# Low halves of the second feed-forward weights from an accumulating transfer instead of a VectorE subtraction

## The chip, the cores and the metric

The kernel runs on one core of a Trainium2 chip. The core has five engines that each follow their own instruction queue: TensorE (PE, matrix products), VectorE (DVE), ScalarE (ACT), GpSimd (POOL) and SyncE (SP, which here only issues transfers). Transfers run on 16 DMA engines. The metric is the device time of one execution in microseconds (us). Before the change it is 1752.12 us, the median of three runs (1749.69 to 1752.14).

## The reference

The program is a two-layer diffusion backbone in 32-bit floats: 256 latent tokens and 256 context tokens of width 1024. Each layer is a feed-forward sub-layer, an attention sub-layer (latent attention in layer 0, windowed attention in layer 1) and a second feed-forward sub-layer. Cut to what matters here:

```python
def swiglu(h, w_in, w_out):                    # w_in: 1024 x 5632, w_out: 2816 x 1024
    g, u = jnp.split(h @ w_in, 2, axis=-1)
    return (jax.nn.silu(g) * u) @ w_out
...
x  = x  + 0.5 * gate_x * swiglu(modulate(rms_norm(x),  shift_x, scale_x), w_in, w_out)
xc = xc + 0.5 * gate_c * swiglu(modulate(rms_norm(xc), shift_c, scale_c), w_in, w_out)
```

Shift, scale and gate come from two conditioning vectors by a product with large modulation weights. The context stream (xc) is not needed after the attention of layer 1, so the last of the four feed-forward sub-layers works on 256 columns (one stream) instead of 512 (two).

## The kernel before

**Three products for one.** A 32-bit operand is held as two tiles, hi (the operand rounded to a shorter float that PE reads at full rate) and lo (operand minus hi). A product is hi·hi + hi·lo + lo·hi, three matmuls per term (`mm3`, lines 205 to 214; the matmuls are L210, L211 and L212, and only L212 reads the weight's lo half).

**A weight tile's way.** SP loads 128 rows of 1024 or 896 floats (512 or 448 KB) into a raw tile (`weight_raw`, L191, name wraw, 3 buffers in a ring). ACT rounds it into whi (L182, a cast, 4 buffers). DVE subtracts, wlo = wraw - whi (L183, 4 buffers); in some attention places POOL does that instead. PE then reads whi and wlo. A buffer of wraw is free for the next load once the subtraction has read it; a buffer of whi or wlo once PE has used it. `weight` and `weight_split` do this for every weight of the program.

**A feed-forward sub-layer** (`ffn`) goes through three groups of 8, 7 and 7 blocks of the 2816 inner columns. For each block, two weight tiles of 1024 columns (in_win) give the gate and the up half; ACT computes the silu (L416), DVE the product (L418), and ACT and DVE split it into hi and lo (the tiles called r2k in the profile). Then comes the group's `closing`: eight tiles of the second weight (in_wout), one per 128 output rows, each 1024 columns wide in the first group and 896 in the others, so 24 or 21 matmuls per tile. DVE adds each result to the residual (L357). In the last group of a two-stream sub-layer the last two tiles are held and computed one stream after the other; the squares for the next norm are taken by ACT (L236) and added up on POOL (L242).

**Background work.** Beside the first three feed-forward sub-layers, modulation vectors are computed in small steps (`pump`): SP loads 512 KB tiles (modraw, L146, 2 buffers), DVE multiplies and adds them into accumulators (L149, L151, 1024 columns each), and PE sums over partitions (L157). There are none beside the last feed-forward sub-layer.

**What sets the order.** A scheduler puts each engine's instructions into one fixed order when the program is built, and inserts the waits; on the chip each engine follows its order, and a waiting instruction holds up those behind it. Tiles of one name share a ring of buffers, and an instruction that writes to a buffer waits until its former contents have been used.

Of the kernel before, what the change touches and what calls it, by code (L numbers as in the profile page):

```python
# [10 lines left out]
F32 = mybir.dt.float32  # L11
F32R = mybir.dt.float32r
# [5 lines left out]
P = 128  # L18
# [19 lines left out]
def hybrid_backbone_kernel(ctx, tc, t, out):  # L38
# [23 lines left out]

# [1 line left out]
    def load_const(name, shape, dtype=F32):  # L64
# [26 lines left out]

# [1 line left out]
    def mod_columns(l, psA, rows, blocks, dests):  # L93
        """psA [rows, 128 * blocks] has values in row off, for each (off, stream, first column) of dests,
        that belong to the d-tiles from that column on."""
        sA = tmp()
        nc.scalar.copy(sA[:rows, :blocks * P], psA[:rows, :blocks * P])
        yield
        psB = bank()
        vB = psB.rearrange("p (b r) -> p b r", r=P)  # L100
        for b in range(blocks):
            nc.tensor.transpose(vB[:, b, :rows], sA[:rows, b * P:(b + 1) * P], ident[:rows, :rows])  # L102
        for off, s, col in dests:
            nc.vector.tensor_tensor(mod[l][:, s, col:col + blocks], vB[:, :blocks, off], modb[:, l, col:col + blocks], ALU.add)
# [9 lines left out]
    def load_column(k):  # L114
        """Both of layer 0's first chunks for d-tile k, as halves of the rows."""
        raws = [[], []]
        for i in range(2):
            for c in range(2):
                raw = r2k().bitcast(F32)
                nc.sync.dma_start(raw, t["modo"][k, c, i])  # L120
                raws[c].append(raw.rearrange("p (k n) -> p k n", k=4))
        return raws
# [40 lines left out]
    def behind(ins):  # L163
        """Queues a block's instructions of ins's engine behind ins."""
        return tc.issue_after(ins.ins) if ins else nullcontext()
# [11 lines left out]

# [1 line left out]
    def split(hi, lo, src, bias=None, engine=nc.vector):  # L179
        """hi + lo = src (+ bias), each with 12 significant bits."""  # L180
        if bias is None:
            nc.scalar.copy(hi, src)  # L182
            return engine.tensor_tensor(lo, src, hi.bitcast(F32), ALU.subtract)  # L183
        else:
            nc.scalar.activation(hi, src, AF.Identity, bias=bias)  # L185
            return nc.vector.scalar_tensor_tensor(lo, src, bias, hi.bitcast(F32), ALU.add, ALU.subtract)  # L186
# [10 lines left out]
    def weight_split(raw, engine=nc.vector, after=None):  # L197
# [5 lines left out]
        return hi[:, :n], lo[:, :n]  # L203

    def mm3(o, terms, which=None, n=None):
        """o = sum over the n terms of lhsT.T @ rhs, operands given as (hi, lo) pairs; or which terms of it."""
        n = n or len(terms)
        for i in range(n) if which is None else which:
            (ah, al), (bh, bl) = terms[i]
            nc.tensor.matmul(o, lhsT=ah, rhs=bh, start=(i == 0), stop=False)  # L210
            nc.tensor.matmul(o, lhsT=ah, rhs=bl, start=False, stop=False)  # L211
            nc.tensor.matmul(o, lhsT=al, rhs=bh, start=False, stop=(i == n - 1))  # L212
# [4 lines left out]
    def rstd_of(parts, dim, after=None):  # L217
        """1 / sqrt(sum over parts / dim + eps) on every partition; parts are tiles of squares."""
        b = bank()[:, :T]
        for i, p in enumerate(parts):  # L220
            nc.tensor.matmul(b, lhsT=ones, rhs=p, start=(i == 0), stop=(i == len(parts) - 1))
        r = strip()
        nc.scalar.activation(r, b, AF.Sqrt, scale=1.0 / dim, bias=eps)  # L223
        with behind(after):
            nc.vector.reciprocal(r, r)  # L225
        return r

    class Squares:
        """The sum of the squares of all tiles but the last, and the last one's."""

# [13 lines left out]
    def load_table(func, q):  # L244
        """Has ScalarE load func's table as soon as q, a tile of squares, is there."""
        d = small(1)
        nc.scalar.activation(d, q[:, 0:1], func, scale=1.0 if func == AF.Sqrt else -1.0)

    class Sublayer:
        """The modulated input of a sub-layer, one stream after the other, and its first weights."""  # L250

# [58 lines left out]
        def leading(self, s):  # L310
            """The products of the prefetched tiles with one stream, in the order in which its input gets ready,
            and those of the other first tiles."""
            self.product(self.lead[:self.both], s)
            if len(self.streams) > 1 and s == 0:
                self.r[1] = self.rstd(1)
            for i in range(self.both, len(self.first)):
                if i == len(self.lead):
                    ap, size = self.first[i]
                    self.lead.append((weight(ap, size, after=self.end), bank(), size // KT))
                self.product(self.lead[i:i + 1], s)  # L320
# [6 lines left out]
        def products(self, specs):  # L327
            """One bank per weight tile: first the prefetched ones, then the others."""
            for i, (ap, size) in enumerate(specs):
# [10 lines left out]
    class Final(Sublayer):  # L340
        """The final norm of the latent stream."""

# [16 lines left out]

    def closing(tiles, chunk, l, streams, nxt, tail, per_tile=0):  # L360
        """x += gate * product, for each (weight, size, inputs); the last tiles one stream after the other,
        so that the next sub-layer's norm of the first stream runs beside the second's products."""
        w = T * len(streams)
# [5 lines left out]
        for d in range(KT - tail):  # L369
            pump(per_tile)  # L370
            ap, inputs = tiles[d]
            wt = weight(ap, len(inputs) * P)
            o = bank()
            mm3(o[:, :w], terms(wt, inputs, slice(0, w)))
            residual(l, chunk, d, o, streams)
            for s in streams:
                if nxt:
                    nxt.grown(s, d)
# [19 lines left out]

# [1 line left out]
    def ffn_specs(l, which):  # L400
        return [(t["win"][l, which, f, u], 1024) for f in range(NF) for u in range(2)]

    def ffn(sl, nxt, per_tile=0):
# [4 lines left out]
        for g, (f0, f1) in enumerate(GROUPS):  # L408
            gu = []
            for f in range(f0, f1):  # L410
# [12 lines left out]
            closing([(t[f"wout{g}"][l, which, d], gu) for d in range(KT)], 2 + 6 * which, l, streams,  # L423
                    nxt if last else None, 2 if last else 0, per_tile // 2)

# [1 line left out]
    def spread(like, x):  # L427
        return x.rearrange("p (i c) -> p i c", i=2) if len(like.shape) == 3 else x

    def block(e, b):  # L430
        """The b-th block of 128 keys."""
        return e[:, b // 2, b % 2 * P:(b % 2 + 1) * P] if len(e.shape) == 3 else e[:, b * P:(b + 1) * P]
# [5 lines left out]
    def softmax(os, scale, place, sink=None, minus_sink=None):  # L438
        """For each (o, w): exp(scale * o) / (sum of that over a row, and of exp(sink))."""
        n = len(os)  # L440
# [23 lines left out]
    def transposed(es, k0):  # L464
        """Blocks k0 and k0 + 1 of the keys of two query tiles -> (hi, lo) [keys, (block, query)]."""
        b = bank()
# [7 lines left out]
    class Rope:  # L474
        """R[:, :T] = rope of q[:, :T]: the split first, so that its product can come later."""

# [17 lines left out]
    class StackedRope(Rope):  # L494
        """The same of two heads' q, each head's split stacked already."""

# [4 lines left out]
    def stack(dst, R, half, engine=nc.vector):  # L501
        """dst [128, n]: rows of R's half as (hi; lo) for half 0, (lo; hi) for half 1."""
        a = slice(64 * half, 64 * half + 64)
# [12 lines left out]
    def pipeline(n, project, rope, scores, turn, apply, q, e, at={}):  # L516
        """Head h's softmax and splits run beside the products of the heads next to it."""
        for h in range(n):
# [10 lines left out]

# [1 line left out]
    def mla_specs():  # L531
        return [(t["wdown"][m], 1024) for m in (4, 5, 0)] + [(t["wkr"], 512)] + [(t["wdown"][m], 1024) for m in range(1, 4)]

    def mla(sl, nxt):
# [3 lines left out]
        class Normed:  # L538
            """RMS norm of the tiles, as pairs."""

# [153 lines left out]

# [1 line left out]
    def swa(sl, nxt):  # L696
# [47 lines left out]
        def scores(m, *qs):  # L744
# [13 lines left out]
            heads = slice(2 * m, 2 * m + 2)  # L758
            # The context's residual is not needed any more.
            place = (lambda j: tmp()) if m % 2 else (lambda j: x_all[:, 2 * j:2 * j + 2, C])  # L760
# [39 lines left out]

# [1 line left out]
    def load_tmp(name, n):  # L802
# [39 lines left out]
    def lead_products(n, k1):  # L842
        """Those of the first n leading weight tiles with the d-tiles before k1."""
        for k in range(k1):
# [57 lines left out]
def _layout(x, c, ctx, c_ctx, mod_w, mod_b, norm_g, final_norm_g, ffn_w_in, ffn_w_out, mla_w_down, mla_q_norm,  # L902
# [9 lines left out]
    def tiles(w, m):  # L912
        """(K, M * m) -> [M, 128, K / 128, m]: each column tile with its K on partitions."""
        k, n = w.shape
# [63 lines left out]
```

## Time and profile before

| | |
|---|---|
| runs, median (lowest to highest) | 1752.12 us (1749.69 to 1752.14) |
| profiled execution, span from first to last instruction | 1747.8 us |
| median of the runs above that span | 4.3 us |
| PE busy | 1686.9 us, 97% |
| DVE busy | 1093.9 us, 63% |
| ACT busy | 659.6 us, 38% |
| POOL busy | 188.1 us, 11% |
| subtractions for wlo on DVE | 302, 361.6 us |
| mean granted TensorE clock | 0.989 |

The profile is of one execution. "Busy" counts an engine's instructions; a matmul's record overlaps with the next one's, so that PE's pace is better read from the distance between tiles than from the length of one record. A group of the profile stands for all instructions of one line with the same operands: its name gives line, engine, operation, output<-input and shape, then the count, busy time and mean in ns, and after the second bar the idle time of the engine just before them and what ended it. A window's row gives the busy time and the count for each engine in a stretch of time, then the granted clock, the busy share of the DMA engines and what they moved.

### The profile page before, as it was taken

The page shows a single profiled execution, that of the slowest core. Times are in us where ns is not written, and L with a number is a line of the kernel's source. Part 1 is how long each engine was busy: PE and PEld are TensorE (multiplying, and loading weights), DVE is VectorE, ACT ScalarE, POOL GpSimd, SP SyncE. Part 2 cuts the span into 40 slices and gives each one's busy share as a digit, 9 for nine tenths or more (in the row PEclk, how much of TensorE's full clock was granted, in tenths as well). Part 3 has the DMA queues.
Part 4 walks back from the last instruction along what each step waited for, and adds up shares of the span by engine and source line. Part 5 has one row for each costly group of instructions (what it writes and reads, how often), then busy time and mean ns, then how long its engine had stood idle before and what let it go on. Part 6 is the DMA issues. An engine that isn't in the chain of part 4 may idle for free.

```text
span 1747.8 us, 23827 instructions
## 1 busy us (share of the span) xinstructions
PE 1686.9 (97%) x9428; PEld 1438.3 (82%) x9428; DVE 1093.9 (63%) x1608; ACT 659.6 (38%) x1105; POOL 188.1 (11%) x183
## 2 busy tenths in 40 slices
PE   7999999999999999999999999999999989889997
PEld 4688888888788898888888888888888878889997
DVE  4877576646767467856946474635433689755554
ACT  4422222234556353222222342222222566554443
POOL 1000000004132130000000220000000452110001
PEclk9999999999999999999999999999999999999998
DMA  9566455431212126644645245635323221145552
GB/s 340 172 199 192 129 192 179 158 120 55 85 49 73 51 84 201 209 143 155 219 128 166 92 158 168 217 119 159 96 97 94 88 85 37 62 145 181 173 191 95
DMA packets 72831, 242.71 MB, mean 139 GB/s; under 512 B 8848, under 2 KB 10640, under 8 KB 72720
## 3 DMA queue, kind: packets, MB, share of 16 engines
q1 hardware_dynamic: 72720, 241.20, 42.6%
q8 instruction: 74, 1.21, 0.3%
q14 instruction: 37, 0.30, 0.1%
HBM read 240.11 MB, written 1.05 MB: 138 GB/s over the span
## 4 chain that ended last, share of the span: by engine, by line
PE 54%; DVE 5%; issue 1%; ACT 1%; POOL 1%; DMA 0%; POOLq 0%; ACTq 0%; DVEq 0%
PE bank L210 18%; PE bank L211 18%; PE bank L212 18%; DVE small L444 1%; DVE r2k L183 1%; DVE x L461 1%; PE bank L157 1%; DVE tmp L461 0%; DVE wlo L183 0%; DVE strip L225 0%; DVE r2k L506 0%; DVE r2k L512 0%; PE bank L102 0%; POOL r2k L183 0%; DVE small L448 0%
## 5 line engine op out<-in xcount | busy, mean ns | idle before, releaser
L210 PE MATMUL bank<-r2k,whi 128*128 128x512 f32 (+1 forms) x2610 | 918.4, 353 | 9.2 <-ACT r2k L185 4.6
L211 PE MATMUL bank<-r2k,whi 128*128 128x512 f32 (+1 forms) x2610 | 915.5, 351 | 8.1 <-POOL r2k L183 5.7
L212 PE MATMUL bank<-r2k,wlo 128*128 128x512 f32 (+1 forms) x2610 | 912.8, 350 | 4.2 <-POOL wlo L183 2.2
L182 ACT CAST whi<-wraw 128x1024 fp32r<-128x1024 f32 (+1 forms) x313 | 321.6, 1028 | 887.6 <-PE bank L211 527.5
L210 PEld LDWEIGHTS bank<-r2k,whi 128*128 128x128 f32 x2610 | 495.2, 190 | 89.6 <-ACT whi L182 9.2
L211 PEld LDWEIGHTS bank<-r2k,whi 128*128 128x128 f32 x2610 | 496.7, 190 | 76.8 <-POOL r2k L183 8.0
L212 PEld LDWEIGHTS bank<-r2k,wlo 128*128 128x128 f32 x2610 | 496.2, 190 | 69.3 <-POOL wlo L183 3.1
L183 DVE TENSOR_TENSOR wlo<-wraw,whi 128x1024 fp32r<-128x1024 f32 (+1 forms) x302 | 361.6, 1199 | 135.1 <-ACT whi L182 124.9
L151 DVE SCALAR_TENSOR_TENSOR big<-modraw,conds,big 128x1024 f32<-128x1024 f32 x196 | 242.4, 1279 | 11.3 <-DMA modraw<-in_modw 10.7
L357 DVE SCALAR_TENSOR_TENSOR x<-bank,mod,x 128x256 f32<-128x256 f32 x192 | 85.7, 478 | 181.7 <-PE bank L212 181.6
L242 POOL TENSOR_TENSOR strip<-strip 128x256 f32<-128x256 f32 x64 | 66.3, 1049 | 1137.0 <-ACT strip L236 1110.3
L418 DVE TENSOR_TENSOR tmp<-bank,tmp 128x512 f32<-128x512 f32 (+1 forms) x88 | 54.9, 623 | 180.3 <-PE bank L212 178.5
L183 DVE TENSOR_TENSOR r2k<-bank,r2k 128x512 fp32r<-128x512 f32 (+2 forms) x107 | 61.1, 615 | 15.6 <-ACT r2k L182 15.3
L182 ACT CAST r2k<-bank 128x512 fp32r<-128x512 f32 (+2 forms) x107 | 51.5, 545 | 15.2 <-PE bank L212 14.8
L183 DVE TENSOR_TENSOR r2k<-tmp,r2k 128x512 fp32r<-128x512 f32 (+1 forms) x88 | 54.3, 618 | 1.5 <-ACT r2k L182 1.4
L182 ACT CAST r2k<-tmp 128x512 fp32r<-128x512 f32 (+1 forms) x88 | 49.7, 566 | 9.7 <-DVE tmp L418 9.2
L416 ACT ACTIVATE tmp<-bank 128x512 f32<-128x512 f32 (+1 forms) x88 | 47.3, 537 | 6.5 <-PE bank L212 6.5
L444 DVE TENSOR_REDUCE small<-bank 128x1 f32<-128x512 f32 (+1 forms) x64 | 37.2, 612 | 0.2 <-PE bank L640 0.2
L236 ACT ACTIVATE strip<-x 128x256 f32<-128x256 f32 x80 | 30.5, 410 | 17.9 <-DVE x L357 17.0
L225 DVE RECIPROCAL strip<-strip 128x256 f32<-128x256 f32 x14 | 24.5, 1750 | 19.9 <-ACT strip L223 19.9
L186 DVE SCALAR_TENSOR_TENSOR r2k<-r2k,mod 128x256 fp32r<-128x256 f32 x45 | 29.9, 688 | 8.8 <-ACT r2k L185 8.6
L450 ACT ACTIVATE tmp<-bank,small 128x512 f32<-128x512 f32 x32 | 21.8, 687 | 30.1 <-DVE small L448 13.0
(150 smaller groups left out, 1057.2 us busy)
## 6 DMA issues: line engine op xcount, KB each, us to landing
wraw<-in_win SPq DMA_DIRECT2D x172, 512.0 KB, 3.5
modraw<-in_modw SPq DMA_DIRECT2D x128, 512.0 KB, 4.2
wraw<-in_wout SPq DMA_DIRECT2D x64, 448.0 KB, 3.3
wraw<-in_wout SPq DMA_DIRECT2D x32, 512.0 KB, 3.5
r2k<-in_modo SPq DMA_DIRECT2D x32, 256.0 KB, 5.8
wraw<-in_mwo SPq DMA_DIRECT2D x8, 512.0 KB, 3.5
wraw<-in_swq SPq DMA_DIRECT2D x8, 512.0 KB, 3.4
wraw<-in_swo SPq DMA_DIRECT2D x8, 512.0 KB, 3.4
```

The costliest lines, as they stand in the source:

```text
L151: nc.vector.scalar_tensor_tensor(acc[s], raw, conds[:, kt, s:s + 1], acc[s], ALU.mult, ALU.add)
L182: nc.scalar.copy(hi, src)
L183: return engine.tensor_tensor(lo, src, hi.bitcast(F32), ALU.subtract)
L210: nc.tensor.matmul(o, lhsT=ah, rhs=bh, start=(i == 0), stop=False)
L211: nc.tensor.matmul(o, lhsT=ah, rhs=bl, start=False, stop=False)
L212: nc.tensor.matmul(o, lhsT=al, rhs=bh, start=False, stop=(i == n - 1))
L236: nc.scalar.activation(q, x, AF.Square)
L242: nc.gpsimd.tensor_tensor(self.parts[0], self.parts[0], q, ALU.add)
L357: nc.vector.scalar_tensor_tensor(xs[d][:, SL[s]], o[:, SL[s]], mod[l][:, s, c:c + 1], xs[d][:, SL[s]], ALU.mult, ALU.add)
L416: nc.scalar.activation(sg[:, :w], og[:, :w], AF.Silu)
L418: nc.vector.tensor_tensor(pr[:, :w], ou[:, :w], sg[:, :w], ALU.mult)
L444: nc.vector.tensor_reduce(top[:, j:j + 1], o[:, :w], axis=AX.X, op=ALU.max)
```

## The change

A second way of making a weight's pair is added, `weight_added`, and the closings of the feed-forward sub-layers use it for all tiles that are not held: 4 x 3 x 8 less 3 x 2, which is 90 tiles (32 of 1024 columns, 58 of 896). ACT casts raw into whi as before; ACT then writes -whi into wlo; then POOL issues a transfer that adds the raw tile onto wlo. The result is again raw - whi. All other weights keep the subtraction. Comments and docstrings are dropped, and what stands below line 204 moves down by 10 lines: the matmuls are L220, L221 and L222 afterwards, the residual L367, the silu L426, the square L246, the adds of squares L252.

```diff
+    def weight_added(ap, n=1024):
+
+        raw = weight_raw(ap, n)
+        hi = ring.tile([P, 1024], F32R, tag="whi", name="whi", bufs=4)
+        lo = ring.tile([P, 1024], F32R, tag="wlo", name="wlo", bufs=4)
+        nc.scalar.copy(hi[:, :n], raw)
+        nc.scalar.mul(lo[:, :n], hi[:, :n].bitcast(F32), -1.0)
+        nc.gpsimd.dma_start(lo[:, :n].bitcast(F32), raw, accum_op=ALU.add)
+        return hi[:, :n], lo[:, :n]
...
-    def closing(tiles, chunk, l, streams, nxt, tail, per_tile=0):
+    def closing(tiles, chunk, l, streams, nxt, tail, per_tile=0, added=False):
...
-            wt = weight(ap, len(inputs) * P)
+            wt = (weight_added if added else weight)(ap, len(inputs) * P)
...
             closing([(t[f"wout{g}"][l, which, d], gu) for d in range(KT)], 2 + 6 * which, l, streams,
-                    nxt if last else None, 2 if last else 0, per_tile // 2)
+                    nxt if last else None, 2 if last else 0, per_tile // 2, added=True)
```

The scheduler's order of the loads on SP, in the second group of the last feed-forward sub-layer. What an instruction waits for stands in brackets: DMAHW is an earlier load, DMASW an earlier accumulating transfer, the other names are engines (the number behind belongs to the semaphore's name). Before:

```order
L191 DMA wraw<-in_wout 128x896 [waits DMAHW0_49,DVE_49]
L191 DMA wraw<-in_wout 128x896 [waits DMAHW1_49,DVE_49]
L191 DMA wraw<-in_wout 128x896 [waits DMAHW2_49,DVE_49]
L191 DMA wraw<-in_wout 128x896 [waits DMAHW3_49,DVE_49]
L191 DMA wraw<-in_wout 128x896 [waits DMAHW4_49,DVE_49]
```

And with the change:

```order
L191 DMA wraw<-in_wout 128x896 [waits DMAHW0_49,DVE_49]
L191 DMA wraw<-in_wout 128x896 [waits DMAHW1_49,DVE_49]
L191 DMA wraw<-in_wout 128x896 [waits DMAHW2_49,DVE_49]
L191 DMA wraw<-in_wout 128x896 [waits DMAHW3_49,DMASW2_49,Activation_49]
L191 DMA wraw<-in_wout 128x896 [waits DMAHW4_49,DMASW3_49,Activation_49]
```

The order of the loads is the same; from the fourth tile on, a load into a raw buffer waits for an accumulating transfer (DMASW) where it waited for DVE.

ACT's order at the same place, where the last two blocks' silu and split run beside the closing's first weights. Before:

```order
L182 CAST whi<-wraw 128x896
L416 ACTIVATE tmp<-bank 128x256
L182 CAST whi<-wraw 128x896
L182 CAST r2k<-tmp 128x256
L182 CAST whi<-wraw 128x896
L416 ACTIVATE tmp<-bank 128x256
L182 CAST whi<-wraw 128x896
L182 CAST r2k<-tmp 128x256
```

And with the change:

```order
L210 CAST whi<-wraw 128x896
L426 ACTIVATE tmp<-bank 128x256
L211 ACTIVATE wlo<-whi 128x896
L210 CAST whi<-wraw 128x896
L182 CAST r2k<-tmp 128x256
L211 ACTIVATE wlo<-whi 128x896
L210 CAST whi<-wraw 128x896
L426 ACTIVATE tmp<-bank 128x256
L211 ACTIVATE wlo<-whi 128x896
L210 CAST whi<-wraw 128x896
L182 CAST r2k<-tmp 128x256
```

A negation (L211) stands behind every cast of a second weight (now L210), and the silu (L426) and the split of the last blocks (the casts into r2k) stand between them as before.

## The prediction

> **What bounds the kernel now.** I read the busy times first, then the groups of instructions by shape, then the table of windows, then single stretches of the timeline.
>
> ```profile
> span 1747.8 us, 23827 instructions
> PE 1686.9 (97%) x9428; PEld 1438.3 (82%) x9428; DVE 1093.9 (63%) x1608; ACT 659.6 (38%) x1105; POOL 188.1 (11%) x183
> ...
> q1 hardware_dynamic: 72720, 241.20, 42.6%
> ...
> L183 DVE TENSOR_TENSOR wlo<-wraw,whi 128x1024 fp32r<-128x1024 f32 (+1 forms) x302 | 361.6, 1199 | 135.1 <-ACT whi L182 124.9
> ...
> wraw<-in_wout SPq DMA_DIRECT2D x64, 448.0 KB, 3.3
> wraw<-in_wout SPq DMA_DIRECT2D x32, 512.0 KB, 3.5
> ```
>
> PE is busy for 97% of the span; all its idle time is 1747.8 - 1686.9 = 60.9 us. The 302 subtractions on DVE look like a large target, but what counts is whether PE waits for them:
>
> ```profile
> L212 PE MATMUL bank<-r2k,wlo 128*128 128x512 f32 x1606 | 626.8, 390 | 4.2 <-POOL wlo L183 2.2 <-DVE wlo L183 2.0
> L211 PE MATMUL bank<-r2k,whi 128*128 128x256 f32 x996 | 286.1, 288 | 7.2 <-POOL r2k L183 5.7 <-DVE r2k L186 1.4
> L212 PE MATMUL bank<-r2k,wlo 128*128 128x256 f32 x996 | 282.9, 285 | 0.0
> ```
>
> In the whole program PE waits 2.0 us for a low half from DVE. The second feed-forward weights (tensors in_wout) are used in twelve closings; the windows show nine of them. Columns: busy time (and count) of PE, weight load, DVE, ACT, POOL, then clock, DMA share, GB/s.
>
> ```profile
> 131.00:176.00 45.00, 45.00 (x205) 36.30 (x204) 32.48 (x43) 9.45 (x11) 0.00 (x0) 1.00 0.61 193
> 256.00:294.00 38.00, 38.00 (x171) 31.46 (x170) 30.89 (x42) 7.88 (x9) 0.00 (x0) 1.00 0.67 206
> 722.00:767.00 45.00, 45.00 (x205) 36.30 (x204) 32.97 (x43) 9.64 (x10) 0.00 (x0) 1.00 0.61 197
> 847.00:885.00 38.00, 38.00 (x171) 31.41 (x170) 31.29 (x43) 7.62 (x10) 0.00 (x0) 1.00 0.64 204
> 1103.00:1147.00 44.00, 44.00 (x196) 35.23 (x195) 22.78 (x33) 8.60 (x9) 1.06 (x1) 1.00 0.56 181
> 1226.00:1264.00 38.00, 38.00 (x170) 31.19 (x169) 15.13 (x26) 7.41 (x8) 0.65 (x1) 1.00 0.33 101
> 1592.00:1614.00 22.00, 21.98 (x184) 21.77 (x183) 13.15 (x17) 7.87 (x8) 0.00 (x0) 1.00 0.55 178
> 1655.00:1675.00 20.00, 19.98 (x167) 19.77 (x166) 13.15 (x17) 7.75 (x9) 0.00 (x0) 1.00 0.60 191
> 1715.50:1735.50 20.00, 19.97 (x163) 19.36 (x161) 9.59 (x14) 6.62 (x13) 6.05 (x6) 1.00 0.20 65
> ```
>
> PE is full in every one of them, so a lighter DVE has nothing to give there. The question is only whether the new path is fast enough. The pace it must hold is read from the residuals, one per tile; the first rows are from a two-stream closing, the others from the last, one-stream, feed-forward:
>
> ```profile
> 756.65 0.88 DVE L357 SCALAR_TENSOR_TENSOR x<-bank,mod,x 128x256 f32<-128x256 f32 x2 [3.35 <-PE bank L212]
> 762.09 0.88 DVE L357 SCALAR_TENSOR_TENSOR x<-bank,mod,x 128x256 f32<-128x256 f32 x2 [3.36 <-PE bank L212]
> ...
> 1593.43 0.48 DVE L357 SCALAR_TENSOR_TENSOR x<-bank,mod,x 128x256 f32<-128x256 f32 x1 [0.60 <-PE bank L212]
> 1596.31 0.48 DVE L357 SCALAR_TENSOR_TENSOR x<-bank,mod,x 128x256 f32<-128x256 f32 x1 [0.64 <-PE bank L212]
> ...
> 1659.15 0.94 ACT L182 CAST whi<-wraw 128x896 fp32r<-128x896 f32 x1 [1.45 <-PE bank L211]
> 1659.23 0.48 DVE L357 SCALAR_TENSOR_TENSOR x<-bank,mod,x 128x256 f32<-128x256 f32 x1 [0.41 <-PE bank L212]
> 1660.12 1.09 DVE L183 TENSOR_TENSOR wlo<-wraw,whi 128x896 fp32r<-128x896 f32 x1 [0.41 <-ACT whi L182]
> 1661.75 0.48 DVE L357 SCALAR_TENSOR_TENSOR x<-bank,mod,x 128x256 f32<-128x256 f32 x1 [0.53 <-PE bank L212]
> ```
>
> A tile takes PE 5.44 us with two streams (7/8 of it, 4.76, where the tile has 896 columns), but with one stream 2.88 us (1024 columns) or 2.52 us (896). ACT casts a tile when PE frees its slot of whi: with 4 slots, three tiles ahead of PE.
>
> **The change part by part.** *Removed:* 90 of the 302 subtractions on DVE, about 90 x 1.2 = 107 us of DVE. Worth 0: PE waits 2.0 us for all 302 together, and not in these windows. *Added on ACT:* 90 negations as wide as the cast. The trace has none; its nearest rows are the cast itself and an activation and a cast of equal width:
>
> ```profile
> L182 ACT CAST whi<-wraw 128x1024 fp32r<-128x1024 f32 x248 | 260.6, 1051 | 682.0 <-PE bank L211 431.3 <-issue 221.0 <-DMA wraw<-in_win 22.1
> L182 ACT CAST whi<-wraw 128x896 fp32r<-128x896 f32 x64 | 60.4, 944 | 205.6 <-issue 109.5 <-PE bank L211 96.1
> L182 ACT CAST r2k<-tmp 128x512 fp32r<-128x512 f32 x66 | 41.0, 622 | 9.7 <-DVE tmp L418 9.2
> L416 ACT ACTIVATE tmp<-bank 128x512 f32<-128x512 f32 x66 | 38.9, 589 | 6.5 <-PE bank L212 6.5
> ```
>
> So between 0.95 and 1.0 of the cast; I take the cast's 1.05 and 0.94 us. ACT goes from 7.75 to about 15.3 of 20 us in the window at 1655: not full. *Added on POOL and the DMA engines:* 90 accumulating transfers of 448 or 512 KB, from the raw tile into the negated one, issued by POOL. POOL is 11% busy, and its adds of squares, which now stand behind transfers, are wanted only at a sub-layer's end: 0.
>
> *What the transfer holds.* The raw tile has 3 buffers. Before, one came free 2.2 us after its cast began (cast and subtraction). Now it is held until the transfer has landed, and SP, which issues in order, waits for that; behind it stand the next weight and modulation loads.
>
> Call D the time from the end of the negation to the landing. A buffer then turns round in load + cast + negation + D + about 0.2 us of handing over: 3.3 + 0.94 + 0.94 + D + 0.2 = 5.4 + D us (896 columns), 3.5 + 1.05 + 1.05 + D + 0.2 = 5.8 + D (1024). Tiles 0 to 2 of a closing are loaded early; every later one waits for the buffer of the tile three before it. So tile 7, the last, descends from tile 1 in two turns. Counted from the cast of tile 0, tile 1 is cast at 2.88 us (PE is still in 1024-column products), ready at 2.88 + 0.94 + 0.94 + 0.1 + D, and tile 7 is ready two turns later: 4.86 + D + 2 x (5.4 + D) = 3 D + 15.7 us. PE would reach it at 3 x 2.88 + 7 x 2.52 = 26.3. The loss of a one-stream closing is therefore **3 D - 10.6 us**, and none under D = 3.5. With 1024 columns: 2.88 + 1.05 + 1.05 + 0.1 + D + 2 x (5.8 + D) - 10 x 2.88 = **3 D - 12.1**, none under 4.0. The tiles after it are made by DVE as before and find a filled ring.
>
> *The size of D.* No row shows an accumulating transfer, nor one issued by POOL. From below: an ordinary load of this size, 3.3 us (3.5). Its parts: q1 needed 42.6% of 1747.8 us for 241.20 MB, 3.09 us per MB, so 1.42 us for 448 KB and 1.62 for 512; the other 1.9 us are fixed. An accumulation has to read both operands, so I count the queue time twice. One load lands in each tile's time and shares the engines: once more. The issue by POOL I put at 0.7, twice SP's, as POOL takes twice DVE's time for one subtraction:
>
> ```profile
> L183 POOL TENSOR_TENSOR wlo<-wraw,whi 128x1024 fp32r<-128x1024 f32 x11 | 27.2, 2497 | 8.9 <-ACT whi L182 7.2 <-PE bank L212 1.1 <-POOL r2k L506 0.4
> L183 DVE TENSOR_TENSOR wlo<-wraw,whi 128x1024 fp32r<-128x1024 f32 x237 | 291.3, 1231 | 115.1 <-ACT whi L182 105.3 <-PE bank L221 3.2 <-PE bank L469 0.6
> L191 SPq DMA_DIRECT2D wraw<-in_wout x96: 327/328/328, 100.2 to 1719.6; - x96
> ```
>
> D = 1.9 + 0.7 + 3 x 1.42 = 6.9 us, and 7.5 for 1024 columns. From above: two reads and a write each at full price and two loads in the way, 1.9 + 0.7 + 5 x 1.42 = 9.7 (10.7). I take the middle, since of the two reads and the shared load none can be argued away.
>
> The Trainium skill, "Collectives: The Full Stack", section on the bandwidth ceiling, says that a reduce moves at half a copy's rate because it needs two source reads, not because the add costs anything; that is the double price that I took.
>
> *The sum.* One-stream closings: 3 x 7.5 - 12.1 = 10.4, and twice 3 x 6.9 - 10.6 = 10.1: 31 us. Two-stream closings: PE takes 4.76 us or more, so three tiles are 14.3; a turn is 5.4 + 6.9 = 12.3, and with a modulation load of 1.6 us in the way of both transfers about 14.8, with 14.3 - 10.4 = 3.9 us of lead to spend: 0. Against the profiled execution that is 1747.8 + 31 = 1779 us of span; the median of the runs lies 4.3 us above that span, which gives **1783 us**.
>
> **The rivals.** *(1) The transfer is as quick as a load, and all is hidden:* D = 3.3 to 4, loss 0 to 3 us, **1752 us**. For it: in the one-stream windows the DMA share is only 0.55 to 0.60. Against: an accumulation moves more than a load, and the share leaves room for less than one double read per tile (0.4 x 2.52 = 1.0 us). The Trainium skill, "DMA: Bandwidth & Descriptors", section on the anatomy of one DMA, gives 2.0 us plus bytes over 436 GB/s for a plain transfer issued by GpSimd, 3.05 us for 448 KB; by that rule this rival holds. No run so far shows it for an accumulating one.
>
> *(2) The DMA engines become the bound in the two-stream closings as well.* Five windows above have a share of 0.56 to 0.67 because the modulation loads run there; 8 transfers of 2.8 or 3.2 us (two reads each) add about 0.6 and go beyond 1. With D = 9.7 plus a modulation load (11.3), and loads at 4.2 as the modulation's own (modraw, below), a turn is 17.6 against 14.3: two turns cost 6.6 less 1.1 of lead, 5.5 us, five times 27. With 19 + 19 + 20 in the last feed-forward that is 84 us: **1836 us**. It decides from a turn of 14.3 us, D about 8.
>
> ```profile
> modraw<-in_modw SPq DMA_DIRECT2D x128, 512.0 KB, 4.2
> ```
>
> *(3) Faster:* low halves of DVE stand on the chain that ended last, and without 90 of them DVE serves what else PE waits for sooner.
>
> ```profile
> PE bank L210 18%; PE bank L211 18%; PE bank L212 18%; DVE small L444 1%; DVE r2k L183 1%; DVE x L461 1%; PE bank L157 1%; DVE tmp L461 0%; DVE wlo L183 0%; DVE strip L225 0%; DVE r2k L506 0%; DVE r2k L512 0%; PE bank L102 0%; POOL r2k L183 0%; DVE small L448 0%
> ```
>
> Their share rounds to 0%, below 0.5% or 8.7 us; if half of that were second feed-forward weights and D under 3.5, **1748 us**. Against: the windows show PE full wherever those weights are used.
>
> **How the numbers follow.** The forecast 52% (own range 1766 to 1803, D from 5 to 9), rival 1 17%, rival 2 26%, rival 3 5%. The range reaches into rivals 1 and 2: 1753 to 1828. A measurement here tells about 0.2%, 3.5 us, from no change. Faster is rival 3: 0.05; same is rival 1 but for its upper end: 0.14; slower 0.81.
>
> **What would show it.** In the changed profile: PE waits for wlo or whi in the windows of the last feed-forward, some 10 us in each closing, in lumps of 3 to 5 us at the fourth and the seventh tile; PE full in the two-stream closings; SP's loads of in_wout waiting for a DMA, not DVE; about 107 us less DVE and 90 us more ACT. PE full at the end would make rival 1 right; waits before 1500 us, rival 2. If the landing time listed for the transfer is not 6 to 8 us, the size of the loss is wrong though the place may be right.

## The result and the profile after

The changed kernel takes **1809.26 us** (median of 4 runs, 1805.49 to 1814.87). The kernel before, run beside it, takes 1750.9 us (1749.39 to 1752.14). The ratio is 1.0338, with a 95% interval from 1.0326 to 1.035: slower by 58.4 us. The profiled executions differ by the same amount, 1806.2 against 1747.8 us of span.

The page of the changed kernel, by the lines that answer to those shown of before:

```profile
PE 1707.7 (95%) x9428; PEld 1452.8 (80%) x9428; DVE 997.1 (55%) x1518; ACT 742.2 (41%) x1195; POOL 262.6 (15%) x273
...
q1 hardware_dynamic: 72720, 241.20, 40.1%
q0 software_dynamic: 12960, 43.39, 12.9%
...
L221 PE MATMUL bank<-r2k,whi 128*128 128x512 f32 (+1 forms) x2610 | 922.6, 354 | 24.4 <-DVE r2k L183 16.7
L222 PE MATMUL bank<-r2k,wlo 128*128 128x512 f32 (+1 forms) x2610 | 918.9, 353 | 16.9 <-DMA wlo<-wraw 12.8
...
L151 DVE SCALAR_TENSOR_TENSOR big<-modraw,conds,big 128x1024 f32<-128x1024 f32 x196 | 242.4, 1280 | 69.7 <-DMA modraw<-in_modw 69.2
L212 POOL DMA_DIRECT2D wlo<-wraw x90 | 78.4, 871 | 1090.3 <-ACT wlo L211 1066.2
...
wlo<-wraw POOLq DMA_DIRECT2D x58, 448.0 KB, 5.5
wlo<-wraw POOLq DMA_DIRECT2D x32, 512.0 KB, 6.5
```

DVE has 97 us less work and ACT 83 us more (forecast: about 107 and 90). The transfers are priced here for the first time. Their queue (q0) was busy 12.9% of 1806.2 us for 43.39 MB, which is 5.4 us per MB; the loads (q1) took 3.0. So an accumulation costs 1.8 times as much per byte. It lands a median of 5.5 us (448 KB) or 6.5 us (512 KB) after its issue.

Two new waits of PE stand in these lines: 12.8 us for the transfer itself, and 16.7 us for a *DVE* split, r2k. The second has nothing to do with low halves of weights. On DVE, 69.2 us are spent waiting for modulation loads (modraw).

The time went in both kinds of closings. Below are five stretches of 60 us around two-stream closings of the changed kernel. The columns are busy time and count of PE, weight load, DVE, ACT and POOL, then the clock, the DMA share and GB/s:

```profile
120.00:180.00 60.00, 56.80 (x244) 45.51 (x243) 35.36 (x45) 19.27 (x21) 6.01 (x7) 0.94 0.89 242
240.00:300.00 60.00, 55.01 (x241) 44.18 (x240) 38.30 (x48) 19.68 (x23) 7.19 (x8) 0.97 0.87 241
720.00:780.00 60.00, 57.07 (x250) 45.87 (x250) 34.88 (x46) 20.09 (x22) 6.88 (x8) 0.97 0.90 256
860.00:920.00 60.00, 57.00 (x252) 44.91 (x251) 34.94 (x48) 18.47 (x21) 4.65 (x5) 0.97 0.79 233
1100.00:1160.00 60.00, 57.39 (x254) 45.95 (x253) 26.05 (x35) 22.50 (x25) 8.95 (x10) 1.00 0.88 259
sum 300.00, PE 283.27 PEld 226.42 DVE 169.52 ACT 100.01 POOL 33.68; mean PE 56.65 PEld 45.28 DVE 33.90 ACT 20.00 POOL 6.74
```

Before, PE was full in these closings at a clock of 1.00. Now it is idle for 300 - 283.3 = 16.7 us. The clock below 1.00 costs about another 0.06 x 56.8 + 0.03 x (55.0 + 57.1 + 57.0) = 8.5 us. Together that is some 25 us of the 58. Most of the rest lies in the three one-stream closings at the end.

**How a two-stream closing loses time.** The chain of waits of the changed kernel in the second of these closings (start, us, what):

```profile
256.91 10.14 DMA modraw<-in_modw
...
267.15 2.48 DVE big L151 x2
269.63 0.61 DVE r2k L183
...
270.29 0.52 PE bank L221
```

A modulation load takes 10.14 us to land; the median of all 128 is 4.3. DVE, which works in order, stands at the multiplication that needs it. Behind that stands the low half of the last block's activations (r2k), and PE waits for this half. No low half of a weight is late here.

**How a one-stream closing loses time.** The chain in the first of the three, and the three rows of PE's timeline in that closing that have a wait (in brackets, us of idle time and what ended it):

```profile
1613.03 0.95 ACT wlo L211
...
1614.27 7.09 DMA wlo<-wraw
...
1621.42 6.30 DMA wraw<-in_wout
...
1627.79 1.06 ACT whi L210
1628.87 1.07 ACT wlo L211
1629.94 0.28 issue
1630.22 6.76 DMA wlo<-wraw
```

```profile
1619.53 0.38 PE L220 MATMUL bank<-r2k,whi 128*128 128x256 f32 x1 [2.34 <-ACT r2k L182]
1627.60 0.39 PE L222 MATMUL bank<-r2k,wlo 128*128 128x256 f32 x1 [1.11 <-DMA wlo<-wraw]
1637.03 0.58 PE L222 MATMUL bank<-r2k,wlo 128*128 128x256 f32 x1 [3.41 <-DMA wlo<-wraw]
```

This is the turn of a raw buffer: transfer, load into the freed buffer, cast, negation, transfer. The first wait is a relative of the two-stream one. ACT stood for 4.14 us at the cast of the fourth tile, whose load was late, and the cast of the last block's activations stood behind it on ACT:

```profile
1618.12 1.04 ACT L210 CAST whi<-wraw 128x1024 fp32r<-128x1024 f32 x1 [4.14 <-DMA wraw<-in_wout]
1619.07 0.40 ACT L182 CAST r2k<-tmp 128x256 fp32r<-128x256 f32 x1
```

After the wait of 3.41 us PE runs at half its clock for about 5 us. The windows of 4 us at that place, with the clock in the third column from the right:

```profile
1634.00:1638.00 4.00, 0.97 (x4) 0.97 (x5) 0.00 (x0) 2.10 (x2) 1.60 (x2) 0.75 1.06 210
1638.00:1642.00 4.00, 4.00 (x21) 4.00 (x20) 0.00 (x0) 0.41 (x1) 0.00 (x0) 0.50 1.01 238
```

In the second window PE is "busy" all the time, but makes 21 matmuls where the kernel before, with 184 in 22 us, makes 33 in that time. In the next 4 us the clock reads 0.90, then 1.00 again. The busy column alone does not show this loss; the clock and the counts do.

### The profile page after: what moved, and what is told of

It reads as the page before. It is cut to its first block, busy times and chain, and to the rows that moved or that the text cites. A ratio compares the mean times of both kernels' runs of the same rounds, so it can differ in the third digit from the quotient of the medians.

```text
span 1806.2 us, 24089 instructions
## 1 busy us (share of the span) xinstructions
PE 1707.7 (95%) x9428; PEld 1452.8 (80%) x9428; DVE 997.1 (55%) x1518; ACT 742.2 (41%) x1195; POOL 262.6 (15%) x273
## 3 DMA queue, kind: packets, MB, share of 16 engines
q0 software_dynamic: 12960, 43.39, 12.9%
## 4 chain that ended last, share of the span: by engine, by line
PE 76%; DVE 8%; DMA 8%; ACT 3%; issue 3%; POOL 2%; SPq 0%; POOLq 0%; DVEq 0%; ACTq 0%
PE bank L221 24%; PE bank L220 24%; PE bank L222 24%; DMA wlo<-wraw 3%; DMA modraw<-in_modw 2%; DMA wraw<-in_wout 1%; DVE r2k L183 1%; DVE big L151 1%; DVE small L454 1%; POOL r2k L183 1%; PE bank L157 1%; POOL r2k L297 1%; DVE x L471 1%; DVE r2k L300 1%; DMA r2k<-in_modo 1%
## 5 line engine op out<-in xcount | busy, mean ns | idle before, releaser
L221 PE MATMUL bank<-r2k,whi 128*128 128x512 f32 (+1 forms) x2610 | 922.6, 354 | 24.4 <-DVE r2k L183 16.7
L220 PE MATMUL bank<-r2k,whi 128*128 128x512 f32 (+1 forms) x2610 | 924.5, 356 | 16.9 <-ACT r2k L182 9.3
L222 PE MATMUL bank<-r2k,wlo 128*128 128x512 f32 (+1 forms) x2610 | 918.9, 353 | 16.9 <-DMA wlo<-wraw 12.8
L220 PEld LDWEIGHTS bank<-r2k,whi 128*128 128x128 f32 x2610 | 499.7, 192 | 98.5 <-ACT r2k L182 11.4
L221 PEld LDWEIGHTS bank<-r2k,whi 128*128 128x128 f32 x2610 | 501.5, 192 | 95.8 <-DVE r2k L183 19.9
L222 PEld LDWEIGHTS bank<-r2k,wlo 128*128 128x128 f32 x2610 | 501.4, 192 | 83.7 <-DMA wlo<-wraw 13.8
L182 ACT CAST whi<-wraw 128x1024 fp32r<-128x1024 f32 (+1 forms) x223 | 233.2, 1046 | 580.7 <-PE bank L221 294.2
L183 DVE TENSOR_TENSOR wlo<-wraw,whi 128x1024 fp32r<-128x1024 f32 (+1 forms) x212 | 259.2, 1226 | 132.0 <-ACT whi L182 122.4
L151 DVE SCALAR_TENSOR_TENSOR big<-modraw,conds,big 128x1024 f32<-128x1024 f32 x196 | 242.4, 1280 | 69.7 <-DMA modraw<-in_modw 69.2
L212 POOL DMA_DIRECT2D wlo<-wraw x90 | 78.4, 871 | 1090.3 <-ACT wlo L211 1066.2
L210 ACT CAST whi<-wraw 128x896 fp32r<-128x896 f32 (+1 forms) x90 | 88.4, 982 | 268.7 <-PE bank L221 231.7
L367 DVE SCALAR_TENSOR_TENSOR x<-bank,mod,x 128x256 f32<-128x256 f32 x192 | 85.5, 477 | 198.7 <-PE bank L222 198.7
L252 POOL TENSOR_TENSOR strip<-strip 128x256 f32<-128x256 f32 x64 | 65.1, 1029 | 181.7 <-ACT strip L246 155.0
L211 ACT ACTIVATE wlo<-whi 128x896 fp32r<-128x896 f32 (+1 forms) x90 | 88.8, 986 | 1.5
L182 ACT CAST r2k<-tmp 128x512 fp32r<-128x512 f32 (+1 forms) x88 | 49.5, 564 | 17.1 <-DVE tmp L428 17.1
L426 ACT ACTIVATE tmp<-bank 128x512 f32<-128x512 f32 (+1 forms) x88 | 47.4, 538 | 7.0 <-PE bank L222 7.0
L246 ACT ACTIVATE strip<-x 128x256 f32<-128x256 f32 x80 | 31.2, 410 | 19.1 <-DVE x L367 18.3
```

Source lines behind the costliest of these rows:

```text
L151: nc.vector.scalar_tensor_tensor(acc[s], raw, conds[:, kt, s:s + 1], acc[s], ALU.mult, ALU.add)
L210: nc.scalar.copy(hi[:, :n], raw)
L211: nc.scalar.mul(lo[:, :n], hi[:, :n].bitcast(F32), -1.0)
L212: nc.gpsimd.dma_start(lo[:, :n].bitcast(F32), raw, accum_op=ALU.add)
L252: nc.gpsimd.tensor_tensor(self.parts[0], self.parts[0], q, ALU.add)
L367: nc.vector.scalar_tensor_tensor(xs[d][:, SL[s]], o[:, SL[s]], mod[l][:, s, c:c + 1], xs[d][:, SL[s]], ALU.mult, ALU.add)
```

## The experiments

The theory after this reading had three parts. In the one-stream closings a raw buffer turns round too slowly (**buffer theory**). In the two-stream closings modulation loads are late and hold up DVE's queue (**order theory**). The rival to both is the **engine theory**: the DMA engines simply have more to move per tile than PE's time for a tile allows. All kernels below were timed in three rounds beside the kernel before, whose median was 1749.9 us for the first four runs, 1750.6 for the next four and 1750.3 for the last four.

### One kind of closing at a time

```diff
-                    nxt if last else None, 2 if last else 0, per_tile // 2, added=True)
+                    nxt if last else None, 2 if last else 0, per_tile // 2, added=len(streams) == 1)
```

> The transfer is used only in the last, one-stream, feed-forward; the two-stream closings have the subtraction back. If the one-stream loss stands by itself, the time is 1751 + 31 to 34 = 1782 to 1785 us (the landmarks of the changed profile put 31.4 us between the residual at the end of the attention and the last residual, and 2.6 behind it). If part of it was carried over from the two-stream closings (a ring still emptied, another order), it is under 1775.

Measured: 1781.59 us, ratio 1.0181 [1.0166, 1.0196], **+31.7 us** for 24 tiles. The counterpart, with `len(streams) == 2`:

> The transfer is used only in the three two-stream feed-forwards. By the landmarks they lose 6.0 + 6.9 + 3.6 + 4.9 + 1.9 = 23 us and the attention one more: 1774 us. If the two losses were not independent, the two runs' losses do not add up to the 58 us of the whole change.

Measured: 1776.85 us, ratio 1.0153 [1.0138, 1.0169], **+27.0 us** for 66 tiles. The two add up to 58.7, against 58.4 for the whole change. So they are separate losses, and each can be studied alone.

### The negation without the transfer

ACT casts and negates as in the changed kernel, but DVE adds the raw tile onto the negated one:

```diff
-        nc.gpsimd.dma_start(lo[:, :n].bitcast(F32), raw, accum_op=ALU.add)
+        nc.vector.tensor_tensor(lo[:, :n], lo[:, :n].bitcast(F32), raw, ALU.add)
```

> ACT casts and negates as in the change, but DVE adds the raw tile onto the negated one, without a transfer. If the transfer alone costs the time, 1748 to 1754 us, like the kernel before. If the 90 negations on ACT hold up casts and silus, 1760 us or more.

Measured: 1748.87 us, ratio 0.9995 [0.9985, 1.0004]. The 90 negations on ACT cost nothing; the whole loss comes with the transfer. (DVE still has one instruction per tile here, so this run says nothing of a lighter DVE.)

### The order on DVE

The whole change, but no modulation step beside a group's last block, and those of the closing queued behind that block's low half (`done`) on DVE:

```diff
-                pump(per_tile // 2, done)
+                pump(per_tile // 2 if f < f1 - 1 else 0, done)
...
-                pump(per_tile - per_tile // 2, done)
+                pump(per_tile - per_tile // 2 if f < f1 - 1 else 0, done)
...
-            pump(per_tile)
+            pump(per_tile, after)
```

> The whole change, but no modulation step is recorded beside the last block of a group, and those of the closing are queued on DVE behind the last block's low half. Order theory (the two-stream closings lose time because DVE, in order, waits for a late modulation load while the last block's low half stands behind it): the waits of PE for that low half go, the two-stream loss falls from 23 to under 8 us, 1786 to 1794 us. Engine theory (the DMA engines have more to move than there is time for, whatever the order): the loss only moves to another wait, 1803 us or more.

Measured: 1786.63 us, ratio 1.0207 [1.019, 1.0224], +36.8. Of the 27 us of the two-stream closings 22 are gone. The first of the five windows above, and the sum of all five, in this kernel:

```profile
120.00:180.00 60.00, 60.00 (x271) 48.73 (x270) 32.57 (x44) 20.48 (x22) 6.00 (x7) 1.00 0.85 238
...
sum 300.00, PE 299.47 PEld 241.15 DVE 165.19 ACT 94.06 POOL 26.10; mean PE 59.89 PEld 48.23 DVE 33.04 ACT 18.81 POOL 5.22
```

PE is full again at a clock of 1.00, though the DMA share in the first window is nearly what it was before the reordering (0.85 against 0.89; it is 0.71 to 0.86 in all five, against 0.79 to 0.90). So DMA engines that busy did not alone stop PE there. What stopped it was what stood behind the late loads. The loads are still late in this kernel, as DVE's wait for them shows (62.0 us against 69.2), but PE's waits for the low half of r2k, 16.7 us before, have left its row:

```profile
DVE big L151 <- DMA modraw<-in_modw: 62.0, 22, 5.9
...
L221 PE MATMUL bank<-r2k,whi 128*128 128x512 f32 (+1 forms) x2610 | 918.0, 352 | 9.5 <-POOL r2k L183 6.1
```

A control asks whether that order is simply better. It is the kernel before with the same three edits and no transfer:

> The kernel before, with only the later modulation steps of the run that lost 36.8 us instead of 58. If those steps' order matters only because the accumulating transfers make the modulation loads late, nothing changes: 1747 to 1753 us. If the order is better in itself, 1730 to 1745 us, and the recovery of 22 us is not a proof of the order theory.

Measured: 1749.32 us, ratio 0.9994 [0.9985, 1.0003]. It is not better in itself; it only matters when modulation loads are late.

### Why the modulation loads are late

SP issues loads in order, and some of its weight loads now wait for an accumulation. If that is what makes modulation loads late, they should be on time when another engine issues them. The control, without any transfer, and the run with two-stream transfers only:

```diff
-            nc.sync.dma_start(raw, t["modw"][l, c, kt])
+            nc.scalar.dma_start(raw, t["modw"][l, c, kt])
```

> The kernel before, with the modulation loads issued by ACT instead of SP: the control for the next run. Their landing is not what any engine waits for there, so both theories expect 1747 to 1756 us; more if ACT, in order, is now held at an issue by a buffer that is not free.

Measured: 1751.72 us, ratio 1.0007 [0.9998, 1.0017].

> The transfer in the two-stream closings only, as in the run that lost 27.0 us, with the modulation loads issued by ACT instead of SP. If those loads are late because they stand behind waiting weight loads in SP's queue, they are now free of them, and the loss against the control falls to 5 to 10 us. If they are late because the DMA engines are full, they are as late from any queue: 20 to 27 us stay.

Measured: 1768.96 us, ratio 1.0103 [1.0086, 1.0121]. Against the control that is +17.2, between the two forecasts. The trace says more than the time. For each kernel, DVE's wait for modulation loads, PE's wait for r2k, and the time to landing of all 128 modulation loads. First SP issuing:

```profile
DVE big L151 <- DMA modraw<-in_modw: 63.9, 27, 6.8
...
PE bank L221 <- DVE r2k L183: 18.3, 7, 3.9
...
DMA to landing us min/median/max: 3.3/4.2/9.5
```

Then ACT issuing:

```profile
DVE big L151 <- DMA modraw<-in_modw: 66.0, 27, 6.1
...
PE bank L221 <- DVE r2k L183: 6.5, 7, 2.4
...
DMA to landing us min/median/max: 3.3/4.3/9.1
```

In total DVE waits as much for these loads: 66.0 against 63.9 us at L151, and 74.1 against 78.2 with the first multiplications (L149). The slowest load takes 9.1 against 9.5 us *after* its issue; in the control the maximum is 6.7. So most of the lateness arises after the issue, on the DMA engines, whichever engine issues. The Trainium skill, "DMA: Bandwidth & Descriptors", section "Issuing engines are not separate DMA queues", says that transfers started by any engine run on the same 16 DMA engines and interleave there; the trace agrees, with 9.1 against 9.5 us.

But the total hides where it matters. PE's long waits for r2k stand at the last block of five groups, one in each of the five stretches above; they sum to 17.1 us with SP issuing and to 5.3 with ACT issuing. In front of four of these five, SP issued a modulation load 2.2 to 3.7 us after its buffer came free, because it stood at a weight load that waited for an accumulation. The first of them, with SP issuing: SP's wait between 124 and 132 us, the issue, and DVE's multiplication that needs the load:

```profile
SPq L191 <- DMA wlo<-wraw: 5.1, 1, 5.1
...
130.81 1.15 SPq L146 DMA_DIRECT2D modraw<-in_modw  x1
...
137.45 1.29 DVE L151 SCALAR_TENSOR_TENSOR big<-modraw,conds,big 128x1024 f32<-128x1024 f32 x1 [2.85 <-DMA modraw<-in_modw]
```

The same load and multiplication with ACT issuing:

```profile
128.51 0.33 ACTq L146 DMA_DIRECT2D modraw<-in_modw  x1
...
137.27 1.27 DVE L151 SCALAR_TENSOR_TENSOR big<-modraw,conds,big 128x1024 f32<-128x1024 f32 x1
```

In the first run the buffer is free at 127.3 us and the load is issued at 130.8; in the second it is free at 128.5 and issued at once, and DVE does not wait there. With ACT issuing, all of these loads follow their free buffer within 0.2 us. So both theories hold in part: SP's order makes loads late just where PE waits, and the landing on busy engines does the rest. How the 27 us divide is not shown. Some loads in front of these waits also landed sooner with ACT issuing (in the fifth group, without any delay at the issue, after 7.3 instead of 8.0 us). And the run has waits of its own, because ACT is now held at the issue of modulation loads: its casts of second weights wait 41.6 us for DVE to free a modulation buffer, and PE waits 2.8 us for the transfer.

### More raw buffers in the one-stream closings

Transfers in the one-stream closings only. Raw tiles rotate over six buffers that are idle at that time (four accumulators, two for modulation loads):

```diff
...
+        i = turn_of[0] % 6
+        turn_of[0] += 1
+        spare = ring.tile([P, 1024], F32, tag="modraw", name="modraw", bufs=2) if i % 3 == 2 else big().bitcast(F32)
-        raw = weight_raw(ap, n)
+        raw = weight_raw(ap, n, spare)
```

> Transfer in the one-stream closings only, as in the run that lost 31.7 us, but their raw tiles rotate over six buffers that lie idle in that stage (the accumulators' and the modulation loads') instead of the three that all weights share. Buffer theory (a closing loses time because a raw buffer turns round too slowly): tile 7 descends from tile 1 in one turn, ready 10.3 + 2 D = 24 us after the first cast at D = 7, before PE's 26.3, so nothing is lost: 1750 to 1756 us. Engine theory (a load and an accumulation take the DMA engines longer than PE takes for a tile: 1.38 + 2.46 = 3.84 against 2.52 us by the queues' shares): no buffer helps but for a few loads pulled ahead, 6 to 8 us stay in each closing, 1768 to 1774 us.

Measured: 1760.96 us, ratio 1.0059 [1.0044, 1.0074], +10.4: between the two theories. Buffers account for 21 of the 31.7 us, and 10.4 stay. To see what stays, the same kernel with a plain copy in place of the accumulation:

```diff
-        nc.gpsimd.dma_start(lo[:, :n].bitcast(F32), raw, accum_op=ALU.add)
+        nc.gpsimd.dma_start(lo[:, :n].bitcast(F32), raw)
```

> As the run with six idle raw buffers in the one-stream closings, but the transfer copies instead of adding; the low half is then the whole weight and no longer what is left over. It asks what the 10.4 us are that six buffers leave. If the DMA engines' time per tile sets them, a copy at 1.6 / 3.8 of the accumulation's share takes 1.1 instead of 2.5 us, with the load 2.5 against PE's 2.52: 1750 to 1754 us. If it is the length of a tile's chain (load, cast, negation, issue, landing), which a copy shortens by some 1.6 us only, 1757 to 1761 us.

Measured: 1751.71 us, ratio 1.0007 [0.9998, 1.0017], +1.4. The window of the first one-stream closing in the run with three buffers, with six, and with six and a copy; the last row of each fence is the transfers' queue (packets, MB, share of the span):

```profile
1570.00:1620.00 50.00, 43.82 (x327) 43.04 (x326) 11.42 (x20) 24.01 (x29) 7.00 (x8) 0.90 0.82 204
...
q0 software_dynamic: 3456, 11.54, 3.8%
```

```profile
1570.00:1620.00 50.00, 45.97 (x373) 44.74 (x372) 16.06 (x24) 26.91 (x32) 7.00 (x8) 1.00 0.88 236
...
q0 software_dynamic: 3456, 11.54, 3.4%
```

```profile
1570.00:1620.00 50.00, 48.53 (x405) 48.33 (x404) 17.81 (x27) 28.49 (x34) 4.41 (x8) 1.00 0.72 250
...
q0 software_dynamic: 2432, 11.54, 1.6%
```

At the pace of the kernel before (184 matmuls in 22 us) 50 us hold 418; here they hold 327, 373 and 405. With six buffers the DMA share rises from 0.82 to 0.88, the clock from 0.90 to 1.00. With a copy the share falls to 0.72, and PE is nearly full. An accumulation takes 3.4% of 1759.1 us for 24 tiles, 2.5 us of the engines each; the copy takes 1.6% of 1750.4, 1.2 us. With a load of 1.4 us beside it that is 3.9 against 2.6 us per tile, where PE needs 2.52 (896 columns) to 2.88 (1024). So more buffers bring back 21 us, and the shorter transfer another 9.

What the 9 us are is less certain than the forecast supposed. These are ACT's waits before its casts of the 24 tiles, with three buffers and then with six:

```profile
ACT whi L210 <- DMA wraw<-in_wout: 35.6, 15, 4.3
```

```profile
ACT whi L214 <- PE bank L225: 24.1, 24, 2.2
```

With three buffers 15 casts wait for a load, which confirms the buffer theory. With six, no cast waits for a load: all 24 wait for PE to free a slot of whi. So the engines do bring the raw tiles in time, and only the accumulation comes late. With 4 slots a tile has three tiles of PE's time, 7.6 or 8.6 us; cast, negation and issue take 2.2 or 2.4 of them, which leaves 5.4 or 6.3 us. The accumulations land after a median of 6.8 us (at most 10.2), the copies after 5.0. The landing is longer where the engines are busier (a median of 5.4 us with three buffers, where the window above has a share of 0.82; 6.8 with six, at 0.88). A fifth slot for whi and wlo might hide it, but no run tries that, so it stays open whether the share or the slots set the 9 us.

### Half the transfer, and a copy, with three buffers

Three buffers again: the transfer makes only the left half of the columns and DVE the right half:

```diff
-        nc.scalar.mul(lo[:, :n], hi[:, :n].bitcast(F32), -1.0)
-        nc.gpsimd.dma_start(lo[:, :n].bitcast(F32), raw, accum_op=ALU.add)
+        h = n // 2
+        nc.scalar.mul(lo[:, :h], hi[:, :h].bitcast(F32), -1.0)
+        nc.gpsimd.dma_start(lo[:, :h].bitcast(F32), raw[:, :h], accum_op=ALU.add)
+        nc.vector.tensor_tensor(lo[:, h:n], raw[:, h:], hi[:, h:n].bitcast(F32), ALU.subtract)
```

> As the one-stream run, but the transfer makes the low half of the left half of the columns only, and DVE subtracts the right half. Buffer theory: D falls by half the accumulation's time on the queue, to 5.8 us; 3 D - 10.6 = 6.8 us stay per closing: about 1770 us. Engine theory: 1.38 + 1.23 = 2.61 us of the DMA engines per tile against 2.52 of PE: 1750 to 1755 us.

Measured: 1767.22 us, ratio 1.0099 [1.0084, 1.0114], +16.7. And a copy of the whole tile:

> As the one-stream run, but the transfer copies the raw tile instead of adding it; the low half is then the whole weight and no longer what is left over, all else is as before. It prices the second read. If the accumulation costs twice a copy on the queue, its share falls from 5.4 to about 3 us per MB and its landing by about 1.1 us; buffer theory: D = 5.9, 7 us per closing, about 1771 us; engine theory: 1.38 + 1.4 = 2.8 us per tile against 2.52, about 2 us per closing, 1756 us. If the issue by POOL is what costs, nothing changes: 1781 us.

Measured: 1766.19 us, ratio 1.0087 [1.007, 1.0104], +15.6. A load and a transfer now need 2.8 us of the engines per tile with the half transfer and 2.6 with the copy, hardly more than PE; still 16 us are lost. The buffer theory said 1770 and 1771, the engine theory 1750 to 1756. This is the same answer from the other side: when the engines nearly have the time, the turn of three buffers still costs some 5 us per closing.

### Both remedies at once

> The whole change with both remedies at once: the modulation steps queued later, as in the run that lost 36.8 us, and in the one-stream closings the six idle raw buffers of the run that lost 10.4. If these are two separate causes, the losses add: 10.4 + (36.8 - 31.7) = 15.5 us, 1763 to 1769 us. If both only spread one shortage of DMA time, one remedy takes from the other: 1772 us or more.

Measured: 1766.4 us, ratio 1.009 [1.0075, 1.0105], +16.1, within the sum of two separate causes. With the order on DVE mended and six buffers, the change costs 16 us instead of 58. No version was faster than the kernel before, and the runs show why none should be expected: with DVE's work taken away PE gains nothing (it was full already), and each transfer adds about 2.5 us to engines that must also load.

## Why the prediction was right, and where it was not

The direction held, and 1809 us lies within the range of 1753 to 1828; but it lies 26 us above the forecast of 1783 and 6 us above the upper end of that case's own range (1803). The miss is the two-stream closings. Step by step:

- **"Removed ... worth 0" and the negations on ACT at 0:** right. With the negations and no transfer the time is 1748.87 us against 1749.86. That run keeps DVE's share; where DVE's 24 instructions are gone and the transfer is a copy with six buffers, the time is 1751.71 us against 1750.27, so nothing is gained.
- **One-stream closings, 31 us:** measured +31.7 alone. The mechanism, a raw buffer held until the transfer has landed, is shown by the runs with six buffers and with half a transfer. But the exact size is partly luck. D was forecast at 7.5 us for 1024 columns; the chain shows 0.28 + 7.09 = 7.4. A turn was forecast at 5.8 + 7.5 = 13.3 us; by the starts of the negations of tiles 1, 4 and 7 of that closing, counted from 0 (1610.08, 1623.41 and 1635.67 us), it was 13.3 and 12.3. But the tile that PE waited for longest was the sixth, tile 5, whose turn on the chain (1613.03 to 1628.87) took 15.8 us because its load took 6.30 instead of 3.5. The sum left out the half-speed PE and the wait behind ACT's queue (2.34 us); and about 9 of the 31.7 us are not the turn of a raw buffer, since more buffers do not bring them back.
- **"An accumulation has to read both operands, so I count the queue time twice":** 1.8 times a load's price per byte, 2.1 times a copy's of the same tiles (3.4% against 1.6%). Nearly right.
- **"Two-stream closings: 0":** this is the step that failed; it cost 27.0 us. The turn of the raw buffers was compared with PE's 14.3 us, and that comparison may stand: PE waited there for r2k, not for wlo, and with the order mended only 5 us are lost. What the sum left out are the modulation loads. The text counted them as something in the transfers' way, and never asked what happens when *they* come late: they hold DVE, and behind them stands a low half that PE needs at once. The sentence "behind it stand the next weight and modulation loads" named the victim and one of its causes, SP's order: PE's five waits fall from 17.1 to 5.3 us when the loads leave SP's queue. It did not follow the late loads to DVE's queue.
- **Rival 2 (DMA engines bound in the two-stream closings too):** its 27 us met the measured 27.0, by another way. The engines are nearly full there (share 0.79 to 0.90; it had said beyond 1), but PE was full at 0.71 to 0.86 once DVE's order was changed. And its 19 + 19 + 20 = 58 us for the last feed-forward were 31.7; its sum of 84 us was 58.4.
- **Rival 1 (as quick as a load):** refuted. The landing is 5.5 and 6.5 us, not 3.3 to 4. The formula that the prediction quotes from the Trainium skill, "DMA: Bandwidth & Descriptors", section on the anatomy of one DMA, 2.0 us plus bytes over 436 GB/s, gives an estimate of 3.05 us for 448 KB. The accumulating transfer took 5.5, and a copy through the same queue 3.4 with three raw buffers and 4.9 with six. So the formula comes near the quicker copies only, and does not hold for an accumulation.
- **What would show it:** waits at "the fourth and the seventh tile" came at the fourth (1.11 us) and the sixth (3.41); "PE full in the two-stream closings" was wrong.

## What to carry to other kernels

When a transfer is put in place of an engine's instruction, ask three things: how long it holds its source buffer, how late its result lands for the slots that the bound engine has ahead (and how much time of the DMA engines it takes), and which *other* loads it delays, on the DMA engines and in the queue that issues them, with what stands in order behind the instructions that wait for those. Here the three cost some 21, 9 and 22 us (the remaining 5 or so were not traced), and the third hit tiles that the change did not touch. Work taken off an engine that the bound engine never waits for pays for none of it.

## What the runs showed of the hardware that was not expected

**PE's clock halves after short stalls.** After the wait of 3.41 us in the changed kernel the clock read 0.50, and matmuls of 256 columns started 0.21 us apart instead of 0.12 for about 5 us. The Trainium skill, "TensorE: Matmul & The Clock Gate", section "What's actually happening", says that PE falls to half its clock after an idle window of about 3.4 us and rises again after about as long of sustained work; this wait agrees, and the 5 us are somewhat longer. But a shorter wait can do it too. In the run with transfers in the one-stream closings only, the matmul behind a wait of 2.43 us took 0.58 instead of 0.38 us, and the clock of the next 4 us read 0.74:

```profile
1595.79 0.58 PE L220 MATMUL bank<-r2k,whi 128*128 128x256 f32 x1 [2.43 <-ACT r2k L182]
```

```profile
1597.00:1601.00 4.00, 4.00 (x28) 4.00 (x27) 0.59 (x2) 2.10 (x2) 1.22 (x2) 0.74 0.89 176
```

The wait of 2.34 us shown further above left the next matmul at 0.38 us, so no sharp threshold can be read from these runs. In the run with six buffers PE waited 14 times for a transfer in the last sub-layer, at most 1.2 us each, and the clock of the closing shown stayed at 1.00.

```profile
PE bank L226 <- DMA wlo<-big: 6.4, 10, 1.2
...
PE bank L226 <- DMA wlo<-modraw: 2.4, 4, 1.0
```

Waits as short as these, it seems, cost their own length only; a long one costs some us of half speed on top.

**An accumulating transfer from one on-chip tile onto another is dear:** 5.4 us of queue time per MB in the changed kernel (5.2 with six buffers), against 2.4 for a copy of such tiles issued by the same engine and 3.0 for a load, and 0.87 us of POOL to issue one.
